# Splitting one gate column earlier and loading the second half of the output weights inside the gated stage

## The chip, the cores and the metric

The kernel runs on one core of a Trainium2 chip. The metric is the device time of one execution in microseconds, as the median of the runs. The engines that matter are TensorE (PE, with its weight loads as PEld), VectorE (DVE), ScalarE (ACT), GpSimd (POOL) and SyncE (SP, which here only issues transfers). Each works through its own list of instructions in order and waits on semaphores for the others.

## The reference, cut to what matters

One encoder layer over two sequences of 512 tokens with 1024 features, all in float32. The part that the change touches:

```python
y = jax.nn.gelu(lax.map(one_seq, u))
y_ssm = y * jax.nn.sigmoid(y @ w_glu + b_glu)
...
mixed = jax.nn.sigmoid(g_att) * y_att + jax.nn.sigmoid(g_ssm) * y_ssm
x = x + mixed @ w_out
h2 = rms_norm(x, ln2)
return x + jnp.square(jax.nn.relu(h2 @ w_up)) @ w_down
```

## The kernel before

Float32 matrices are multiplied as three products of rounded parts: each operand is kept as a high part (a cast on ACT) and a low part (the remainder, a subtraction on DVE). Making both from a raw tile is called a **split** here; a 256 KB piece (128 x 512) takes one ACT and one DVE instruction.

The **gated stage** (the loop over `u`, 2 to 15) makes `mixed`, transposed, in 16 units: `u = 2m + s` for eight columns `m` of 128 features, counted from 0, and two sequences `s`. For a unit, `product_of` runs 24 matmuls on PE against column `m` of `w_glu` (from unit 4 on; the first four products are made in the attention stage), `gate_out` (ACT, L723) applies the sigmoid, `mixed` (DVE, L728 and L729) multiplies and adds, `gated_states` (DVE, L710 and L711, with a sigmoid L707 on ACT for the later columns) prepares the next unit, and `parts_of` splits the result (ACT L733, DVE L734) into `mixT`. Three accumulators rotate among the products.

Beside this the stage makes two kinds of weights ready. `column_half(c, i)` loads half of column `c` of `w_glu` (SP, L682) into a `c_raw` buffer and splits it (ACT L683, DVE L684) into `gc_hi` and `gc_lo`; there are two buffers of each, so column `c` takes the place of column `c - 2`. `row_piece` loads one of the eight row pieces of a half of `w_out` (SP, L1170), also into one of the same two `c_raw` buffers (named `w_raw`), and splits it (ACT L1171, DVE L1172) into `w_rows`. `load_gates(m)` has POOL issue two 512 KB loads for a later column. Within the stage the order of PE, ACT, DVE, POOL and SP is that of the code.

Behind the stage come the **output products**: `out_half(x1, sq, t, b)` runs 24 matmuls of a token tile against half `b` of `w_rows`, DVE adds the input row (L1238), and `norm_of` (ACT L1255, POOL L1257 and L1258, DVE L1259, which needs `ln2_bc`) and `turn_of` (transposes on PE, L1273) prepare the up projection. PE runs half 0 for both sequences first, then half 1 for both, then the first transposes. Half 1 of `w_rows` is loaded and split at the head of this part, through three `w_raw` buffers of the pool `rn2`, into `slot_a`, where the gated stage keeps the state rows (`yT`) of columns 4 to 7. Two pieces of `w_up` (`f_raw`, L1247 to L1249) go through the same three buffers after that. Here only PE's order is that of the code; a scheduler sets the other engines' order.

Of the kernel before, what the change touches and what calls it, by code (L numbers as in the profile page):

```python
# [12 lines left out]
F32 = mybir.dt.float32  # L13
# [6 lines left out]
P = 128  # L20
D = 1024
# [3 lines left out]
KT = D // P  # L25
NSEQ = 2
HALF = 512
# [36 lines left out]
def hybrid_layer(ctx, tc, x, rel, onehot, w_qkv, w_ug, vectors, lam, coefs, w_glu, w_out, ln2,  # L64
                 w_up, w_down, out):
    nc = tc.nc
    V, S, PE, GP, SP = nc.vector, nc.scalar, nc.tensor, nc.gpsimd, nc.sync
# [58 lines left out]
    def slot(pool):  # L126
        return [pool.tile([P, KT, HALF], F32R, tag=f"act{i}", name=f"act{i}") for i in range(2)]


    slot_a = opers.enter_context(tc.tile_pool(name="slot_a", bufs=1, side="right", reuse_waits="tile"))  # L130
# [5 lines left out]
    cpool = cpool_cm.__enter__()  # L136
# [12 lines left out]
    columns = [("u", U_BLK + c) for c in range(KT)] + [("a", GA_BLK + c) for c in range(KT)] + [("s", GS_BLK + c) for c in range(KT)]  # L149
# [525 lines left out]
    def glu_pieces(m, pool, eng=V):  # L675

        def piece(i):
            if i == 0:
                glu_w[m] = [pool.tile([P, KT, P], F32R, tag=tag, name="g" + tag) for tag in ("c_hi", "c_lo")]
            hi, lo = [q[:, i * KT // 2:(i + 1) * KT // 2, :] for q in glu_w[m]]  # L680
            raw = cpool.tile([P, KT // 2, P], F32, tag="c_raw", name="c_raw")
            SP.dma_start(raw, w_glu[m][:, i * KT // 2:(i + 1) * KT // 2, :])  # L682
            S.copy(hi, raw)  # L683
            return lambda: eng.tensor_tensor(lo, raw, hi.bitcast(F32), op=ALU.subtract)  # L684

        return [lambda i=i: piece(i) for i in range(2)]

    def load_gates(m):
        tiles = [p.tile([P, NTOK], F32, tag=tag, name=name) for p, tag, name in
                 ((wq, "c_hi", "ga"), (wq, "c_lo", "gs"), (evp, "ev", "at"))]  # L690
        glu_in[m] = tiles
        for t_, scr in zip(tiles[1:], (gs_scr, mix_scr)):
            GP.dma_start(t_, scr[m])
# [3 lines left out]
    def column_half(c, i):  # L697
        pieces.setdefault(c, glu_pieces(c, cpool))[i]()()
# [5 lines left out]
    def gated_states(u, pool, tag):  # L704
        m, s, (ga, gs, at) = sides(u)
        if (GS_BLK + m, s) not in sigmoids:
            S.activation(gs, gs, AF.Sigmoid)  # L707
        yy = pool.tile([P, HALF], F32, tag=tag, name="yy")
        halves = [q[:, m % 4].bitcast(F32).rearrange("p (t s k) -> p t s k", t=T, s=NSEQ)[:, :, s, :] for q in yT[m // 4]]
        V.tensor_add(yy.rearrange("p (k t) -> p t k", t=T), *halves)  # L710
        V.tensor_mul(gs, gs, yy)  # L711

    def product_of(u):
        m, s = divmod(u, 2)
        ps = acc()
        for k in range(KT):
            for _ in glu_step(ps, glu_w[m], k, s):
                pass
        glu_ps[m, s] = ps

    def gate_out(u):
        m, s, (ga, gs, at) = sides(u)
        S.activation(ga.rearrange("p (k t) -> p k t", t=T), glu_ps[m, s].rearrange("p (t k) -> p k t", t=T), AF.Sigmoid,  # L723
                     bias=bglu_sb[:, m:m + 1])

    def mixed(u):
        m, s, (ga, gs, at) = sides(u)
        V.tensor_mul(ga, ga, gs)  # L728
        V.tensor_add(ga, ga, at)  # L729

    def parts_of(u):
        m, s, (ga, gs, at) = sides(u)
        S.copy(mixT[s][0][:, m, :], ga)  # L733
        V.tensor_sub(mixT[s][1][:, m, :], ga, mixT[s][0][:, m, :].bitcast(F32))  # L734
# [430 lines left out]
    wpool_cm = tc.tile_pool(name="wpool", bufs=1, side="right", reuse_waits="tile")  # L1165
    wpool = wpool_cm.__enter__()

    def row_piece(w, half, k, raw):

        SP.dma_start(raw, w_out[half, :, k])  # L1170
        S.copy(w[0][:, k], raw)  # L1171
        V.tensor_sub(w[1][:, k], raw, w[0][:, k].bitcast(F32))  # L1172

    w_rows = [slot(wpool), None]
    mixT = [slot(slot_c), slot(slot_d)]
    with tc.tile_pool(name="glu", bufs=1, reuse_waits="tile") as gpool, \
            tc.manual_schedule(engines={ET.PE, ET.Activation, ET.DVE, ET.Pool, ET.SP}):
        parts_of(0)
        parts_of(1)
        load_gates(2)  # L1180
        for u in range(2, 2 * KT):
            m, s = divmod(u, 2)
            if u > 3:
                product_of(u)
                gate_out(u)
            mixed(u)
            if u + 1 < 2 * KT:
                gated_states(u + 1, gpool, "yy")
            parts_of(u)
            if s == 0 and m + 1 < KT:  # L1190
                if m > 2:
                    column_half(m + 1, 1)
                elif m == 1:
                    row_piece(w_rows[0], 0, 0, cpool.tile([P, HALF], F32, tag="c_raw", name="w_raw"))
            if s == 1:
                if m + 2 < KT:
                    if m > 1:
                        column_half(m + 2, 0)
                    load_gates(m + 2)
            if s == 1 and m < 7:  # L1200
                row_piece(w_rows[0], 0, m, cpool.tile([P, HALF], F32, tag="c_raw", name="w_raw"))
            if u == 14:
                row_piece(w_rows[0], 0, 7, cpool.tile([P, HALF], F32, tag="c_raw", name="w_raw"))
    wq_cm.__exit__(None, None, None)
    evp_cm.__exit__(None, None, None)
    cpool_cm.__exit__(None, None, None)
# [3 lines left out]

    t4p_cm = tc.tile_pool(name="t4p", bufs=1, reuse_waits="tile")
    t4p = t4p_cm.__enter__()
    w_rows[1] = slot(slot_a)
    b0, b1, t23 = mixT[0], mixT[1], slot(slot_b)
    t4 = [t4p.tile([P, 4, HALF], F32R, name=f"t4_{i}") for i in range(2)]
    B11, B21 = [[q[:, k:k + 4, :] for q in b0] for k in (0, 4)]
# [5 lines left out]
    first = []  # L1222
    with tc.tile_pool(name="rn2", bufs=2, reuse_waits="tile") as rn2:
        ln2_bc = rn2.tile([P, D], F32, name="ln2_bc", bufs=1)
        SP.dma_start(ln2_bc, ln2.to_broadcast([P, D]))
        for k in range(KT):
            row_piece(w_rows[1], 1, k, rn2.tile([P, HALF], F32, tag="w_raw", name="w_raw", bufs=3))

        def rows_of(sq, t):
            return slice((sq * 4 + t) * P, (sq * 4 + t + 1) * P)  # L1230

        def out_half(x1, sq, t, b):
            ps = acc()
            for k in range(KT):
                mm3(ps, [q[:, k, t * P:(t + 1) * P] for q in mixT[sq]], [q[:, k, :] for q in w_rows[b]],
                    k == 0, k == KT - 1)
            xs = x1[:, b * HALF:(b + 1) * HALF]
            V.tensor_add(xs, ps, xs)  # L1238

        def load_rows_of(sq, t):  # L1240
            x1 = rn2.tile([P, D], F32, tag="x1", name="x1")
            SP.dma_start(x1, x[rows_of(sq, t), :])
            return x1
# [66 lines left out]
        xb, owed = [], None  # L1310
        order.enter_context(tc.manual_schedule(engines={ET.PE}))
        x1s = [load_rows_of(sq, 0) for sq in range(NSEQ)]
        for sq in range(NSEQ):
            out_half(x1s[sq], sq, 0, 0)
        ws = [up_parts(0, i, *[fpre.tile([P, 4, P], F32R, tag=tag, name=tag) for tag in ("f_hi", "f_lo")]) for i in range(2)]
# [27 lines left out]
    with tc.tile_pool(name="up", bufs=2, reuse_waits="tile") as fp:  # L1343
# [43 lines left out]
        for r in range(NPAIR):  # L1387
            raw = fp.tile([P, 4, 4, P], F32, tag="u_raw", name="u_raw")
# [202 lines left out]
```

## Time and profile before

| | |
|---|---|
| median of 3 runs | 1502.4 us (1500.92 to 1504.12) |
| profiled execution | 1503.71 us |
| its span | 1501.9 us |
| granted TensorE clock, mean | 0.998 |
| ACT busy | 761.7 us (51%) |
| POOL busy | 212.6 us (14%) |

The profile is of one execution; its span runs from the first to the last recorded instruction. A row of the timeline has the start, the duration, the engine, the line, the operation with its output and inputs, and, in brackets, how long the engine idled just before and what ended that. A row of the stage sums has a stretch of the span, then the busy time and the number of instructions of each engine in it, the granted clock, the mean busy share of the 16 DMA engines and what they moved in GB/s. SPq rows are transfers that SP issues. Matmuls overlap, so a matmul's duration is longer than the distance to the next one.

### The profile page before, as it was taken

The numbers are of one execution on the slowest core, as the hardware profiler recorded it, in microseconds if no ns is written. First come the engines' busy times: TensorE is split into PE (matmuls) and PEld (weight loads), VectorE is DVE, ScalarE is ACT, GpSimd is POOL, SyncE is SP. The second block draws the span as 40 slices with busy tenths as digits, with TensorE's granted clock in tenths as the row PEclk, the third lists the DMA queues.
The fourth block names the chain that finished last, engine by engine and source line by source line (L and its number), as shares of the span: only waits on it lengthen the run. The fifth ranks groups of instructions, "written<-read, shape, count | busy, mean of one in ns | idle before, by whom it ended". The sixth has DMA issues, their size and how long they took to land.

```text
span 1501.9 us, 22138 instructions
## 1 busy us (share of the span) xinstructions
PE 1453.4 (97%) x8074; PEld 1230.0 (82%) x8074; DVE 1106.8 (74%) x1989; ACT 761.7 (51%) x1362; POOL 212.6 (14%) x372
## 2 busy tenths in 40 slices
PE   6999999999999999999999989999999999999998
PEld 4888888888999888887787868888888888888787
DVE  7998859976646888887975478777777588575653
ACT  6777852235536777775334254445555443433332
POOL 3133341002232443222100000000000000000000
PEclk9999999999999999999999999999999999999999
DMA  4455469229731445275544234444443794454441
GB/s 174 140 169 168 160 208 345 107 100 344 287 132 36 155 135 183 88 252 170 185 135 162 92 115 159 155 154 154 155 154 126 267 352 132 153 182 154 126 123 60
DMA packets 103165, 249.69 MB, mean 166 GB/s; under 512 B 12266, under 2 KB 23786, under 8 KB 103056
## 3 DMA queue, kind: packets, MB, share of 16 engines
q1 hardware_dynamic: 60528, 140.07, 28.7%
q0 software_dynamic: 16896, 53.53, 10.3%
q10 hardware_dynamic: 25632, 54.67, 9.7%
q8 instruction: 64, 1.05, 0.3%
q14 instruction: 45, 0.37, 0.1%
HBM read 173.74 MB, written 90.21 MB: 176 GB/s over the span
## 4 chain that ended last, share of the span: by engine, by line
PE 78%; DVE 8%; ACT 4%; DMA 4%; issue 3%; POOL 1%; ACTq 0%; SPq 0%; DVEq 0%; POOLq 0%
PE acc L185 14%; PE bank L117 13%; PE bank L118 13%; PE bank L116 13%; PE acc L813 4%; PE acc L123 3%; PE acc L117 2%; PE acc L118 2%; PE acc L116 2%; PE sps L547 2%; PE po L896 2%; PE sps L864 1%; PE tps L880 1%; PE sps L645 1%; DMA fac<-rs_scr 1%
## 5 line engine op out<-in xcount | busy, mean ns | idle before, releaser
L185 PE MATMUL acc<-act,c_hi 128*128 128x512 f32 x768 | 249.6, 400 | 1.0 <-DVE act L304 1.0
L117 PE MATMUL bank<-b_lo,a_hi 128*128 128x512 f32 x448 | 174.6, 390 | 1.6 <-DVE b_lo L1460 1.6
L118 PE MATMUL bank<-b_hi,a_lo 128*128 128x512 f32 x448 | 174.3, 389 | 0.0
L116 PE MATMUL bank<-b_hi,a_hi 128*128 128x512 f32 x448 | 173.5, 389 | 0.0
L185 PEld LDWEIGHTS acc<-act,c_hi 128*128 128x128 f32 x768 | 142.2, 189 | 29.1 <-DVE act L304 2.4
L185 PE MATMUL acc<-act,c_lo 128*128 128x512 f32 x384 | 152.5, 397 | 0.0
L1459 ACT CAST a_hi<-d_a 128x1024 fp32r<-128x1024 f32 x56 | 59.0, 1054 | 179.7 <-PE bank L117 176.4
L116 PE MATMUL bank<-act,act 128*128 128x512 f32 x368 | 144.1, 391 | 4.9 <-ACT act L1349 4.9
L117 PE MATMUL bank<-act,act 128*128 128x512 f32 x368 | 143.7, 391 | 0.0
L118 PE MATMUL bank<-act,act 128*128 128x512 f32 x368 | 143.7, 391 | 0.0
L1460 DVE TENSOR_TENSOR a_lo<-d_a,a_hi 128x1024 fp32r<-128x1024 f32 x56 | 68.5, 1224 | 99.9 <-ACT a_hi L1459 99.9
L813 PE MATMUL acc<-w_hi,act 128*128 128x256 f32 x512 | 116.2, 295 | 0.0
L117 PEld LDWEIGHTS bank<-b_lo,a_hi 128*128 128x128 f32 x448 | 84.1, 188 | 20.1 <-DVE b_lo L1460 2.6
L116 PEld LDWEIGHTS bank<-b_hi,a_hi 128*128 128x128 f32 x448 | 84.1, 188 | 17.5
L118 PEld LDWEIGHTS bank<-b_hi,a_lo 128*128 128x128 f32 x448 | 84.1, 188 | 17.3
L813 PEld LDWEIGHTS acc<-w_hi,act 128*128 128x128 f32 x512 | 87.0, 189 | 3.7
L874 ACT ACTIVATE p<-p,nmx 128x257 f32<-128x257 f32 (+1 forms) x128 | 72.1, 563 | 31.2 <-DVE nmx L868 30.2
L116 PEld LDWEIGHTS bank<-act,act 128*128 128x128 f32 x368 | 69.4, 189 | 19.7 <-ACT act L1349 5.3
L123 PE MATMUL acc<-act,gc_hi 128*128 128x512 f32 x256 | 82.6, 401 | 1.8 <-ACT gc_hi L683 1.8
L185 PEld LDWEIGHTS acc<-act,c_lo 128*128 128x128 f32 x384 | 72.4, 189 | 14.0 <-DVE c_lo L176 0.5
L118 PEld LDWEIGHTS bank<-act,act 128*128 128x128 f32 x368 | 69.4, 189 | 14.9 <-DVE act L1350 0.4
L117 PEld LDWEIGHTS bank<-act,act 128*128 128x128 f32 x368 | 69.5, 189 | 14.3
(328 smaller groups left out, 3434.4 us busy)
## 6 DMA issues: line engine op xcount, KB each, us to landing
d_a<-a_scr SPq DMA_DIRECT2D x56, 512.0 KB, 3.6
u_raw<-in_w_up_dram SPq DMA_DIRECT2D x32, 512.0 KB, 5.1
a_scr<-t ACTq DMA_DIRECT2D x64, 256.0 KB, 4.8
k<-in_w_down_dram SPq DMA_DIRECT2D x32, 512.0 KB, 6.4
c_raw<-in_w_ug_dram SPq DMA_DIRECT2D x48, 256.0 KB, 3.7
a_scr<-a ACTq DMA_DIRECT2D x46, 256.0 KB, 2.1
ct_scr<-ctab POOLq DMA_DIRECT2D x16, 576.0 KB, 3.7
ctab_in<-ct_scr POOLq DMA_DIRECT2D x16, 576.0 KB, 7.6
```

The lines of the kernel that those rows point to most:

```text
L116: PE.matmul(ps, a[0], b[0], start=first, stop=False)
L117: PE.matmul(ps, a[0], b[1], start=False, stop=False)
L118: PE.matmul(ps, a[1], b[0], start=False, stop=last)
L123: PE.matmul(ps, w[wi][:, k, :], rows[yi], start=k + p == 0, stop=k == KT - 1 and p == 2)
L185: PE.matmul(ps, w[wi][:, k, :], hT[s][hi][:, k, :], start=n == 0, stop=n == 3 * KT - 1)
L547: PE.matmul(ps[:, i * P:(i + 1) * P], bm[:, ri, g, :], u_sb[:, gp * SH + g, :], start=True, stop=True)
L645: PE.matmul(o, ctab[:, g0 % SI + g, ri, 0:T * CH], st[:, ri, g].rearrange("p s k -> p (s k)"), start=False, stop=ri == 1)
L813: PE.matmul(self.ps, hT[sq][act][:, k, col:col + P], w[:, k % 4, :], start=i == 0, stop=i == 3 * KT - 1)
L874: S.activation(p, p, AF.Exp, bias=self.nmx[:, h:h + 1], scale=-1.0, accum_out=self.sums[:, h, self.qb:self.qb + 1])
L896: PE.matmul(self.po, vv, self.hl[i][part], start=i + part == 0, stop=i == self.nkb - 1 and part == 1)
L1459: S.copy(hi, src)
L1460: V.tensor_sub(lo, src, hi.bitcast(F32))
```

## The change

Column 4, the fifth, is loaded and split in units 3 and 4 instead of 5 and 6; columns 5 to 7 keep their units. The eight row pieces of half 0 move from units 2, 3, 5, 7, 9, 11, 13 and 14 to units 7 to 14, one in each, behind the column's half. Half 1 of the output weights is loaded by the gated stage: pieces 0 to 3 into two tiles of the pool's `c_hi` and `c_lo` buffers, which held a column, issued in unit 13; pieces 4 and 5 through the two small buffers in unit 14, pieces 6 and 7 through them behind that. `w_rows[1]` is taken from `slot_a` in unit 14, and piece 0 is split there, the others behind the last unit. The load of `ln2_bc` moves behind the first loads of `x`.

```diff
-    def row_piece(w, half, k, raw):
-
+    def row_load(half, k, raw):
         SP.dma_start(raw, w_out[half, :, k])
+        return raw
+
+    def row_split(half, k, raw):
+        w = w_rows[half]
         S.copy(w[0][:, k], raw)
         V.tensor_sub(w[1][:, k], raw, w[0][:, k].bitcast(F32))
...
+        columns = {u: (4 + i // 2, i % 2) for i, u in enumerate((3, 4, 7, 8, 9, 10, 11, 12))}
+        late_raw = []
+
+        def small_piece(half, k):
+            return row_load(half, k, cpool.tile([P, HALF], F32, tag="c_raw", name="w_raw"))
+
         for u in range(2, 2 * KT):
...
             parts_of(u)
-            if s == 0 and m + 1 < KT:
-                if m > 2:
-                    column_half(m + 1, 1)
-                elif m == 1:
-                    row_piece(w_rows[0], 0, 0, cpool.tile([P, HALF], F32, tag="c_raw", name="w_raw"))
-            if s == 1:
-                if m + 2 < KT:
-                    if m > 1:
-                        column_half(m + 2, 0)
-                    load_gates(m + 2)
-            if s == 1 and m < 7:
-                row_piece(w_rows[0], 0, m, cpool.tile([P, HALF], F32, tag="c_raw", name="w_raw"))
+            if s == 1 and m + 2 < KT:
+                load_gates(m + 2)
+            if u in columns:
+                column_half(*columns[u])
+            if 7 <= u < 14:
+                row_split(0, u - 7, small_piece(0, u - 7))
+            if u == 13:
+                last = small_piece(0, 7)
+                for tag in ("c_hi", "c_lo"):
+                    pair = cpool.tile([P, 2, HALF], F32, tag=tag, name="w_raws")
+                    for i in range(2):
+                        late_raw.append(row_load(1, len(late_raw), pair[:, i]))
             if u == 14:
-                row_piece(w_rows[0], 0, 7, cpool.tile([P, HALF], F32, tag="c_raw", name="w_raw"))
+                row_split(0, 7, last)
+                late_raw += [small_piece(1, k) for k in (4, 5)]
+                w_rows[1] = slot(slot_a)
+                row_split(1, 0, late_raw[0])
+        for k in range(1, KT):
+            row_split(1, k, late_raw[k] if k < 6 else small_piece(1, k))
...
-    w_rows[1] = slot(slot_a)
...
-        SP.dma_start(ln2_bc, ln2.to_broadcast([P, D]))
-        for k in range(KT):
-            row_piece(w_rows[1], 1, k, rn2.tile([P, HALF], F32, tag="w_raw", name="w_raw", bufs=3))
...
         x1s = [load_rows_of(sq, 0) for sq in range(NSEQ)]
+        SP.dma_start(ln2_bc, ln2.to_broadcast([P, D]))
```

The three places below are from ACT and SP. First ACT at the head of the gated stage, from the cast of unit 2's part on, before:

```order
L733 CAST act_8417<-ga 128x512
L1171 CAST act_8415<-w_raw 128x512
L733 CAST act_8419<-ga 128x512
L1171 CAST act_8415<-w_raw 128x512
L723 ACTIVATE ga<-acc,vec 128x512
L733 CAST act_8417<-ga 128x512
L723 ACTIVATE ga<-acc,vec 128x512
L733 CAST act_8419<-ga 128x512
L683 CAST gc_hi<-c_raw 128x512
```

And in the changed kernel:

```order
L733 CAST act_8417<-ga 128x512
L733 CAST act_8419<-ga 128x512
L683 CAST gc_hi<-c_raw 128x512
L723 ACTIVATE ga<-acc,vec 128x512
L733 CAST act_8417<-ga 128x512
L683 CAST gc_hi<-c_raw 128x512
L723 ACTIVATE ga<-acc,vec 128x512
L733 CAST act_8419<-ga 128x512
L723 ACTIVATE ga<-acc,vec 128x512
```

The two casts of row pieces (L1171) are gone from here, and the two casts of column 4 (L683) stand around `gate_out(4)`, the first L723, where the first of them stood behind `gate_out(5)`.

SP from the last load of a column (L682) to the loads of `f_raw`, before; L1242 loads `x`, L1225 `ln2_bc`:

```order
L682 DMA c_raw<-in_w_glu_dram 128x512
L1170 DMA w_raw<-in_w_out_dram 128x512 x2
L1225 DMA ln_bc<-in_ln_dram 128x1024
L1170 DMA w_raw<-in_w_out_dram 128x512 x3
L1242 DMA x_9000<-in_x_dram 128x1024
L1170 DMA w_raw<-in_w_out_dram 128x512 x3
L1242 DMA x_9002<-in_x_dram 128x1024
L1170 DMA w_raw<-in_w_out_dram 128x512 x2
L1247 DMA f_raw<-in_w_up_dram 128x512 x4
```

And in the changed kernel, where `w_raws` are the two tiles in the column's buffers and the lines are L1169 (row pieces), L1252 (`x`), L1323 (`ln2_bc`) and L1257 (`f_raw`):

```order
L682 DMA c_raw<-in_w_glu_dram 128x512
L1169 DMA w_raw<-in_w_out_dram 128x512 x3
L1169 DMA w_raws<-in_w_out_dram 128x512 x4
L1169 DMA w_raw<-in_w_out_dram 128x512 x2
L1252 DMA x_8997<-in_x_dram 128x1024
L1252 DMA x_8999<-in_x_dram 128x1024
L1169 DMA w_raw<-in_w_out_dram 128x512 x2
L1323 DMA ln_bc<-in_ln_dram 128x1024
L1257 DMA f_raw<-in_w_up_dram 128x512 x4
```

Six of the eight loads of half 1 now stand ahead of the first load of `x`, and `ln2_bc` stands behind all eight.

ACT at the end of the gated stage, from unit 14's part on, before (L723 is `gate_out(15)`, `act_8952` is half 1 of the output weights):

```order
L733 CAST act_8417<-ga 128x512
L1171 CAST act_8415<-w_raw 128x512
L723 ACTIVATE ga<-acc,vec 128x512
L733 CAST act_8419<-ga 128x512
L1171 CAST act_8952<-w_raw 128x512 x8
L1248 CAST f_hi<-f_raw 128x512
```

And in the changed kernel, where `act_8924` is half 1:

```order
L733 CAST act_8417<-ga 128x512
L1174 CAST act_8415<-w_raw 128x512
L1174 CAST act_8924<-w_raws 128x512
L723 ACTIVATE ga<-acc,vec 128x512
L733 CAST act_8419<-ga 128x512
L1174 CAST act_8924<-w_raws 128x512 x3
L1174 CAST act_8924<-w_raw 128x512 x4
L1258 CAST f_hi<-f_raw 128x512 x2
```

One cast of half 1 moved ahead of `gate_out(15)`; the other seven follow the last part as before. From there on the order of every engine is the same, but for the add, the `f_raw` splits and the store of the first `x` rows, which change places by one or two.

## The prediction, on record before the changed kernel ran

> **What bounds the kernel now.** The page was read first (shares of the engines, then the chain that ended last), then the sums by stage around the code that moves, then the timeline of TensorE (PE) there, then the queues that it waits for.
>
> ```profile
> PE 1453.4 (97%) x8074; PEld 1230.0 (82%) x8074; DVE 1106.8 (74%) x1989; ACT 761.7 (51%) x1362; POOL 212.6 (14%) x372
> core 0: us, PE busy (x) PEld busy (x) DVE busy (x) ACT busy (x) POOL busy (x), PEclk, DMA share, GB/s
> 708.79:730.55 21.76, 21.76 (x97) 17.82 (x95) 21.34 (x30) 7.37 (x13) 3.21 (x6) 1.00 0.56 188
> 730.55:741.64 11.09, 8.15 (x25) 5.52 (x25) 10.92 (x17) 5.00 (x10) 1.11 (x3) 0.85 0.68 213
> 741.64:779.76 38.12, 38.12 (x169) 31.53 (x168) 32.59 (x46) 16.97 (x29) 2.16 (x4) 1.00 0.40 132
> 779.76:790.64 10.88, 10.88 (x49) 9.01 (x48) 3.97 (x7) 3.17 (x5) 0.00 (x0) 1.00 0.59 191
> 790.64:804.77 14.13, 12.67 (x49) 8.47 (x47) 7.10 (x12) 5.39 (x9) 0.81 (x2) 1.00 0.68 220
> 806.00:884.00 78.00, 77.93 (x371) 64.40 (x372) 41.36 (x57) 26.27 (x46) 5.56 (x14) 1.00 0.24 88
> ```
>
> PE is busy for 97% of the span, so a change pays only where PE idles or runs slowly. In the gated stage and behind it that is 730.55 to 741.64 (8.15 of 11.09 busy, granted clock 0.85) and 790.64 to 806. Elsewhere there PE is gapless; in the first row VectorE (DVE) is nearly gapless too, 21.34 of 21.76.
>
> ```profile
> 730.32 0.39 PE L123 MATMUL acc<-act,gc_lo 128*128 128x512 f32 x1
> 731.31 0.73 PE L123 MATMUL acc<-act,gc_hi 128*128 128x512 f32 x2 [0.61 <-ACT gc_hi L683]
> 732.78 0.50 PE L123 MATMUL acc<-act,gc_lo 128*128 128x512 f32 x1 [0.73 <-DVE gc_lo L684]
> 736.56 0.73 PE L123 MATMUL acc<-act,gc_hi 128*128 128x512 f32 x2 [1.23 <-ACT gc_hi L683]
> 737.66 0.50 PE L123 MATMUL acc<-act,gc_lo 128*128 128x512 f32 x1 [0.36 <-DVE gc_lo L684]
> 779.08 0.61 PE L123 MATMUL acc<-act,gc_hi 128*128 128x512 f32 x2
> 779.76 0.39 PE L116 MATMUL acc<-act,act 128*128 128x512 f32 x1
> 797.22 0.49 PE L116 MATMUL acc<-act,act 128*128 128x512 f32 x1 [0.57 <-ACT act L1171]
> 805.98 1.09 PE L1273 MATMUL tps<-ident,rn_xn 128*128 128x128 f32 x8 [1.05 <-DVE rn_xn L1259]
> ```
>
> The first four waits are product u=8, the first that reads column 4: both halves of its split come late. From 779.08 to 779.76 three matmuls start, 0.2267 us each, so a product or an output half of 24 takes 5.44.
>
> **The change, part by part.** First, **column 4**. Its load stands behind row pieces that hold the two `c_raw` buffers:
>
> ```profile
> 720.38 0.33 SPq L682 DMA_DIRECT2D c_raw<-in_w_glu_dram  x1
> 732.75 1.01 SPq L682 DMA_DIRECT2D c_raw<-in_w_glu_dram  x2
> 719.67 0.69 DVE L1172 TENSOR_TENSOR act<-w_raw,act 128x512 fp32r<-128x512 f32 x1
> 713.12 0.94 SPq L1170 DMA_DIRECT2D w_raw<-in_w_out_dram  x2
> 742.07 0.69 DVE L1172 TENSOR_TENSOR act<-w_raw,act 128x512 fp32r<-128x512 f32 x1 [0.19 <-ACT act L1171]
> 742.68 0.69 DVE L728 TENSOR_TENSOR ga<-ga,gs 128x512 f32<-128x512 f32 x1
> 743.40 0.69 DVE L729 TENSOR_TENSOR ga<-ga,at 128x512 f32<-128x512 f32 x1
> 744.01 1.14 DVE L710 TENSOR_TENSOR yy<-act,act 128x512 f32<-128x512 f32 x1
> 745.19 0.69 DVE L711 TENSOR_TENSOR gs<-gs,yy 128x512 f32<-128x512 f32 x1
> 745.80 0.69 DVE L734 TENSOR_TENSOR act<-ga,act 128x512 fp32r<-128x512 f32 x1
> ```
>
> The second half is issued at 732.75, after product 8 should have begun. The change puts both loads where the two row loads stand at 713.12. DVE then decides: by the starts above a unit (L728 to L734) takes 3.73 of it and a split 0.61. From 719.67, where the first L1172 drops out, unit 3 with one split and unit 4 up to its split give 719.67 + 4.34 + 3.73 = 727.7, so column 4 is whole at 728.4, 2.1 before PE needs its first half at 730.55. Product 8's wait goes: eight products of 5.44 from 730.55 end at 774.08 instead of 779.76. **Gain 5.68**; bounds: nothing, if column 4 is still late, and 5.68.
>
> Part of that is a slow clock, which has a row of its own:
>
> ```profile
> 738.00:742.00 4.00, 4.00 (x12) 3.14 (x11) 3.81 (x6) 1.72 (x4) 1.08 (x2) 0.57 0.75 226
> 783.00:800.00 17.00, 15.54 (x62) 11.03 (x61) 7.41 (x11) 5.36 (x9) 0.00 (x0) 1.00 0.75 242
> ```
>
> After waits of at most 1.23 us each the clock was granted at 0.57 over 4 us, which costs 4 x 0.43 = 1.7 of the 5.68; the waits between 793 and 798 left it at 1.00. So a short wait that stays could cost 1.7 too, which is a rival below. The Trainium skill ("TensorE: Matmul & The Clock Gate", section "Why this matters for your kernels") asks only that PE has no gaps over about 3 us: by that rule no wait that stays here costs clock and that rival falls away; the row of 738 doesn't bear the rule out.
>
> Second, a **new wait on ScalarE (ACT)**: column 4's first cast now stands ahead of `gate_out(4)` and waits until product 5 has read column 2, whose buffer it takes. That is about 719.6 (730.55 less two products of 5.44, less one matmul).
>
> ```profile
> 722.82 0.68 ACT L723 ACTIVATE ga<-acc,vec 128x512 f32<-128x512 f32 x1
> ```
>
> Behind it stand `gate_out(4)` and the rest of ACT, and DVE and the accumulators wait for those; but `gate_out(4)` runs only at 722.82 now, behind casts of parts that wait for the late DVE. Cost 0; were that cover gone, 0.62, the cast itself.
>
> Third, the **row pieces of half 0** move to units 7 to 13, eight splits as before. Units 7 to 12 then take 3.73 + 1.22 = 4.95 of DVE, under 5.44. But DVE enters late, and column 5's second half shows it: 719.67 + 4.34 + 4.34 + 3.73 + 3.73 + 4.95 + 3.73 = 744.5, done at 745.2, while product 10 asks for it at 730.55 + 10.88 + 3.17 = 744.6. So 0.6 of wait. Its load starts when the first half's split ends, 740.2:
>
> ```profile
> DMA to landing us min/median/max: 2.6/3.1/3.3
> DMA to landing us min/median/max: 2.7/3.2/4.9
> gs<-gs_scr POOLq DMA_DIRECT2D x7, 512.0 KB, 3.6
> ```
>
> (First `c_raw`, then `w_raw`, issue to landing; last one of the two loads that POOL issues for a column, with its median.) With 3.1 and 0.6 of cast it is no later than DVE; with 4.9 the wait is 1.9. **Cost 0.7**, near the median; from 0.6 to 1.9. Later columns have the 0.5 a unit that DVE gains.
>
> Fourth, **half 1 of the output weights**. Now its loads wait for the stage to end, three buffers at a time, and PE catches up with them:
>
> ```profile
> SPq L1225 <- DVE ga L729: 12.8, 1, 12.8
> 783.61 1.28 SPq L1170 DMA_DIRECT2D w_raw<-in_w_out_dram  x3
> 786.79 0.62 ACT L1171 CAST act<-w_raw 128x512 fp32r<-128x512 f32 x1 [3.98 <-DMA w_raw<-in_w_out_dram]
> 799.60 0.62 ACT L1248 CAST f_hi<-f_raw 128x512 fp32r<-128x512 f32 x1 [1.63 <-DMA f_raw<-in_w_up_dram]
> 800.86 0.68 DVE L1238 TENSOR_TENSOR x<-acc,x 128x512 f32<-128x512 f32 x1
> 802.47 1.06 ACT L1255 ACTIVATE rn_xn<-x 128x1024 f32<-128x1024 f32 x1
> 804.64 1.29 DVE L1259 SCALAR_TENSOR_TENSOR rn_xn<-x,rs,ln_bc 128x1024 f32<-128x1024 f32 x1 [1.35 <-POOL rs L1258]
> ```
>
> Four output halves from 779.76 would end at 779.76 + 21.76 = 801.52; the transposes begin at 805.98. The excess of 4.46 is 3.25 of waits for half 1's splits (the fourth half ends at 804.77) and 1.21 for the norm chain, whose add (800.86) and square (802.47) stood behind `f_raw`'s splits. In the change pieces 0 to 3 load into the freed column buffers once product 13 is done (763.2 + 0.7), 4 and 5 by 775. Product 15 ends at 774.8; with piece 0's cast, `gate_out`, two mixes, cast and split (0.62 + 0.68 + 1.33 + 0.62 + 0.69) the last part is done at 778.7, and five splits of 0.61 end at 781.8. Pieces 6 and 7 wait for splits 4 and 5, so issue about 781.5 and land by 786.4 even with 4.9; their splits end by 788, and PE, which reaches half 1 at 774.8 + 10.88 = 785.7, asks for piece 6 at 789.7. `x`, `ln2` and `f_raw` go out between, by about 784; the norm chain (800.86 to 805.93, 4.2 without its late square) fits in the 5.44 of the fourth half. The one cast of half 1 ahead of `gate_out(15)` waits for product 15 and adds 0.62 to a part that PE reads only at the end of the second half, 785. **Gain 4.46**; bounds: nothing, if the loads land as late as the part allows, and 4.46.
>
> **Sum**: 5.68 - 0.70 + 4.46 = 9.4. The profiled execution took 1503.71 (span 1501.9) and would take 1494.3; the median of the runs is 1.3 below it, so 1493.0. From 806 on PE is gapless (77.93 of 78), with the same order on every engine, and the stage moves forward whole.
>
> **The rivals.**
>
> The load loop becomes the bound. In units 7 to 12 each half's load is issued only when the half before is split: landing plus 1.5 (cast, split, three handovers) a turn. At the median, 4.6, it hides under 5.44; at 4.9, the longest row, a turn is 6.4, and five turns from 740.2 end at 772.2 where product 14 asks at 766.4: the gated stage loses 5.8, all that it gained, and 1498.0 is left. For it: POOL's two 512 KB loads and a row piece share those units. Against it: DMA share 0.40 in 741 to 780, no `c_raw` over 3.3. 9%. The Trainium skill ("DMA: Bandwidth & Descriptors", section "Issuing engines are not separate DMA queues") says that transfers of all issuing engines interleave on the same 16 engines, which speaks for it; no row here parts that from the spread of 2.7 to 4.9.
>
> Slower: the same loop with landings above 5.8 us: five turns of 7.3 end at 776.7 and eat all 10.1. At 6.5, 1506. No row has it. 3%.
>
> Column 4 doesn't come early, because something ahead of its casts is later than DVE's count: only 4.46 is left, 1497.9. Its margin is 2.1. 4%.
>
> The wait that stays trips the clock as at 738: 1.7 more, 1494.7. The waits of 793 to 798 speak against it. 5%.
>
> A wait that these rows don't show gives most of it back, say behind 884 where the next stage starts: 1501. The same rows on every engine speak against it. 4%.
>
> **How the numbers follow.** The forecast holds 75%. The low end of the range is 1502.4 - 10.1 (nothing left of the 0.7) less 1.5, by which the runs lie apart from their median: 1490.8. The high end takes in the clock and the load loop for landings up to about 4.8, 1497.6; some 14% is left above it. Same means 1499.4 to 1505.4 (0.2%, about what a measurement of this kernel can tell): 4%, the last case; slower 3%; the other cases are faster, 93%.
>
> **What would show it.** Right: no PE wait for `gc_hi` at product 8 and a clock of 1.00 there; a wait of 0.5 to 1 near 744.5 for column 5; the first output product at 774 to 775.5; no waits for half 1, and transposes at 796 to 797. Wrong: gaps at units 9 to 14 that end with `c_raw` landing, a gap before `tps<-ident,rn_xn`, or 806 to 884 longer than 78.

## The result, and the profile after

The changed kernel took 1492.69 us (median of 4 runs, 1490.92 to 1494.04), against 1503.26 for the kernel before beside it: ratio 0.9927, 95% interval 0.9914 to 0.994. A second comparison (6 runs against 11) gave 1493.45 against 1502.85, ratio 0.994, interval 0.9925 to 0.9956. The forecast was 1493.0, with 1490.8 to 1497.6 as its range.

First the page of the changed kernel and its busy time by stretch; the columns are those of the prediction's first block.

```profile
PE 1448.4 (97%) x8074; PEld 1228.8 (83%) x8074; DVE 1105.0 (74%) x1989; ACT 760.9 (51%) x1362; POOL 212.5 (14%) x372
...
core 0: us, PE busy (x) PEld busy (x) DVE busy (x) ACT busy (x) POOL busy (x), PEclk, DMA share, GB/s
705.40:727.16 21.76, 21.76 (x98) 18.02 (x96) 21.35 (x30) 7.50 (x14) 3.14 (x6) 1.00 0.56 182
727.16:738.04 10.88, 10.88 (x50) 9.01 (x48) 10.71 (x16) 4.01 (x7) 1.16 (x3) 1.00 0.55 199
738.04:749.55 11.51, 11.04 (x49) 8.79 (x48) 11.34 (x17) 5.99 (x10) 1.07 (x2) 1.00 0.65 222
749.55:771.48 21.93, 21.93 (x98) 18.16 (x97) 20.19 (x30) 11.78 (x20) 1.07 (x2) 1.00 0.57 183
771.48:782.36 10.88, 10.88 (x49) 9.01 (x48) 7.38 (x13) 5.23 (x10) 0.00 (x0) 1.00 0.55 189
782.36:793.24 10.88, 10.88 (x49) 8.82 (x47) 4.51 (x7) 2.82 (x5) 0.81 (x2) 1.00 0.54 174
793.24:871.50 78.26, 77.93 (x371) 64.31 (x371) 41.83 (x58) 26.27 (x46) 5.54 (x14) 1.00 0.23 88
```

The second row is products 8 and 9, where PE was busy for 8.15 of 11.09 us at a clock of 0.85 before: now it is gapless at 1.00. Of the waits one is left in the gated stage (738 to 749.55), and the third and fourth output halves (782.36 to 793.24), which lost 3.25 before, are gapless. Now PE's timeline, at the anchors and at that wait.

```profile
699.80 0.27 PE L921 MATMUL tps<-ident,rsum 128*16 128x128 f32 x1 [0.35 <-DVE rsum L916]
...
740.76 0.61 PE L123 MATMUL acc<-act,gc_hi 128*128 128x512 f32 x2
741.84 0.50 PE L123 MATMUL acc<-act,gc_lo 128*128 128x512 f32 x1 [0.47 <-DVE gc_lo L684]
...
771.48 0.39 PE L116 MATMUL acc<-act,act 128*128 128x512 f32 x1
...
793.68 1.09 PE L1283 MATMUL tps<-ident,rn_xn 128*128 128x128 f32 x8 [0.28 <-DVE rn_xn L1269]
```

And the anchor of the kernel before:

```profile
703.19 0.27 PE L921 MATMUL tps<-ident,rsum 128*16 128x128 f32 x1 [0.35 <-DVE rsum L916]
```

The transposes of `rsum` are the last thing that PE does for the attention inside the gated stage, 5.60 us ahead of product 4 in both kernels, and no code ahead of them changed. Yet they ran at 703.19 in one profiled execution and at 699.80 in the other; over the profiled executions below they lie from 699.80 to 705.90, with the same code ahead. So 3.39 of the difference between the two spans is spread from ahead of the change, and **all that follows is measured from this row**: to the first output product (called R-O) and from there to the first transposes of the norm (O-N).

- R-O: 779.76 - 703.19 = 76.57 before, 771.48 - 699.80 = 71.68 after. Gain 4.89.
- O-N: 26.22 before, 22.20 after. Gain 4.02; four gapless output halves are 21.76.
- Together **8.91**, where the prediction summed 9.4.

### The profile page after: what moved, and what is told of

Read it like the earlier page. It is cut to its first block, busy times and chain, and to the rows that moved or that the text cites. A ratio compares the mean times of both kernels' runs of the same rounds, so it can differ in the third digit from the quotient of the medians.

```text
span 1489.1 us, 22131 instructions
## 1 busy us (share of the span) xinstructions
PE 1448.4 (97%) x8074; PEld 1228.8 (83%) x8074; DVE 1105.0 (74%) x1989; ACT 760.9 (51%) x1362; POOL 212.5 (14%) x372
## 3 DMA queue, kind: packets, MB, share of 16 engines
q8 instruction: 64, 1.05, 0.3%
## 4 chain that ended last, share of the span: by engine, by line
PE 76%; DVE 9%; issue 5%; ACT 4%; DMA 4%; POOL 1%; SPq 0%; ACTq 0%; DVEq 0%; POOLq 0%
PE acc L185 14%; PE bank L117 13%; PE bank L118 13%; PE bank L116 13%; PE acc L813 4%; PE acc L123 2%; PE acc L117 2%; PE acc L118 2%; PE acc L116 2%; PE sps L547 2%; PE po L896 2%; PE sps L864 1%; PE tps L880 1%; DVE pl L889 1%; DVE ya L906 1%
## 5 line engine op out<-in xcount | busy, mean ns | idle before, releaser
L116 PEld LDWEIGHTS bank<-act,act 128*128 128x128 f32 x368 | 69.4, 189 | 19.6 <-ACT act L1360 5.3
L185 PEld LDWEIGHTS acc<-act,c_lo 128*128 128x128 f32 x384 | 72.4, 189 | 13.9 <-DVE c_lo L176 0.4
```

The lines of the kernel that those rows point to most:

```text
L116: PE.matmul(ps, a[0], b[0], start=first, stop=False)
L185: PE.matmul(ps, w[wi][:, k, :], hT[s][hi][:, k, :], start=n == 0, stop=n == 3 * KT - 1)
```

## The experiments

The expectations call the stretch from product 4 to the first output product A, and the one from product 4 to the first transposes B: A is R-O less 5.60. They put A and B of the change at 65.91 and 88.11; from the `rsum` row they are 66.08 and 88.28.

| run | R-O | O-N | gained in the stage | ratio (interval) |
|---|---|---|---|---|
| before | 76.57 | 26.22 | | |
| the change, first and second time | 71.68, 71.60 | 22.20, 21.89 | 8.91, 9.30 | 0.9927 (0.9914 to 0.994), 0.994 (0.9925 to 0.9956) |
| 1 columns only | 71.67 | 26.94 | 4.18 | 0.9978 (0.9967 to 0.9989) |
| 2 half 1 only | 76.58 | 21.97 | 4.24 | 0.9963 (0.9949 to 0.9977) |
| 3 row pieces moved, column 4 not | 73.26 | 21.76 | 7.77 | 0.995 (0.9932 to 0.9967) |
| 4 column 4 moved, row pieces not | 73.88 | 21.76 | 7.15 | 0.9961 (0.9947 to 0.9974) |
| 6 row pieces a unit later | 71.01 | 22.14 | 9.64 | 0.9946 (0.9929 to 0.9962) |
| 7 `ln2` later | 71.71 | 21.77 | 9.31 | 0.9935 (0.9921 to 0.9949) |
| 8 both | 71.27 | 21.76 | 9.76 | 0.9936 (0.9921 to 0.9951) |
| 9 one buffer claimed, both in use | 71.57 | 22.05 | 9.17 | 0.9941 (0.992 to 0.9962) |
| 10 column 4's second half in unit 6 | 74.73 | 21.77 | 6.29 | one run |
| 11 the same in unit 7 | 79.04 | 21.76 | 1.99 | one run |
| 12 one buffer | 91.32 | 22.24 | -10.77 | 1.0064 (1.0047 to 1.0081) |

The stage's own gain, read from one execution, lies inside the interval of the times in every row that has one but the first (8.91, where the interval begins at 0.6% of 1503.26, 9.0).

### 1 and 2: the two halves of the change, each alone

Run 1 keeps the columns and row pieces of the change and loads half 1 as before:

```diff
-                for tag in ("c_hi", "c_lo"):
...
-                late_raw += [small_piece(1, k) for k in (4, 5)]
...
+        SP.dma_start(ln2_bc, ln2.to_broadcast([P, D]))
+        for k in range(KT):
+            row_split(1, k, row_load(1, k, rn2.tile([P, HALF], F32, tag="w_raw", name="w_raw", bufs=3)))
```

> Columns and row pieces of half 0 as in the change; half 1 of the output weights loaded behind the stage as before. Two stretches are read: A, from product 4's first matmul to the first output product (70.97 before, 65.91 in the change), and B, from the same start to the first transposes (97.19 and 88.11). Theory (the gains add up): A 65.9, and behind it the 26.22 of before, so B 92.1; time 5.1 below before, ratio 0.9966. Rival (the waits for half 1 came from the late column, so they shrink with it): A 65.9, B 89 to 90, time 7.5 to 9 below before.

Run 2 keeps the loads of half 1 and puts columns and row pieces back:

```diff
-        columns = {u: (4 + i // 2, i % 2) for i, u in enumerate((3, 4, 7, 8, 9, 10, 11, 12))}
+        columns = {u: (4 + i // 2, i % 2) for i, u in enumerate((5, 6, 7, 8, 9, 10, 11, 12))}
+        rows = {2: 0, 3: 1, 5: 2, 7: 3, 9: 4, 11: 5, 13: 6}
...
-            if 7 <= u < 14:
-                row_split(0, u - 7, small_piece(0, u - 7))
+            if u in rows:
+                row_split(0, rows[u], small_piece(0, rows[u]))
```

> Columns and row pieces of half 0 in the units of before; half 1 of the output weights loaded as in the change. Theory (the gains add up): A 71.0 with the four waits at product 8 and the clock of 0.57 near them, then the 22.20 of the change, B 93.2; time 4.0 below before, ratio 0.9973. Rival (half 1's loads in the stage push a wait into products 14 and 15 or the early output halves when the stage is late): A above 71.3 or B above 94, time less than 3 below before.

R-O is 71.67 in run 1, that of the change, and 76.58 in run 2, that of before; O-N of run 2 is 21.97. The two halves are separate, as the prediction had them: 4.90 of R-O and 4.25 of O-N make 9.15, and the change with both has 8.91 and 9.30. B is 98.55 - 5.60 = 92.95 in run 2, where 93.2 was expected. In run 1 it is 93.01, 0.9 more than expected, since O-N is 0.72 longer than before; in time run 1 is 3.5 below before where 5.1 was expected (its ratio of 0.9966 lies just outside the interval), run 2 is 5.7 below where 4.0 was. The window of run 1 behind its waits for half 1 shows what came on top of them (the columns are those of the stage sums):

```profile
795.60:799.30 3.70, 3.40 (x8) 2.45 (x9) 2.19 (x4) 1.48 (x3) 0.00 (x0) 0.54 0.48 137
```

The clock fell to 0.54 behind waits of at most 0.49 each, where waits of up to 0.57 left it at 1.00 in the kernel before. Over 3.7 us that costs 3.7 x 0.46 = 1.7; O-N grew by less, since the gap of 1.05 ahead of the transposes is gone. And run 2 shows the late column 4 again, in PE's timeline:

```profile
729.63 0.73 PE L123 MATMUL acc<-act,gc_hi 128*128 128x512 f32 x2 [0.60 <-ACT gc_hi L683]
731.12 0.50 PE L123 MATMUL acc<-act,gc_lo 128*128 128x512 f32 x1 [0.76 <-DVE gc_lo L684]
...
734.45 0.73 PE L123 MATMUL acc<-act,gc_hi 128*128 128x512 f32 x2 [0.77 <-ACT gc_hi L683]
736.01 0.57 PE L123 MATMUL acc<-act,gc_lo 128*128 128x512 f32 x1 [0.83 <-DVE gc_lo L684]
```

with the clock at 0.51 from 736.30 to 739.80.

### 3 and 4: which move frees column 4

Both have half 1 as in the change. Run 3 has only the first of run 2's edits (`columns` at 5 and 6), run 4 only the second (`rows`).

> As the change, but column 4 stays in units 5 and 6, where it stood before; the row pieces are behind it, from unit 7 on. Theory (the two loading buffers and VectorE's count decide, and the row pieces held both): by a timetable made from the durations of the trace product 8 waits 2.2 in three waits (0.6, 0.25, 1.36), A 67.5, B 89.7, time about 7.5 below before; 1.7 more of each if the clock drops as it did before. Rival (column 4's place in the order alone decides): the waits of before stay, A 71.0, B 93.2, time 4.0 below before.

> As the change, but the row pieces of half 0 stay in their units of before (2, 3, 5, 7, 9, 11, 13, 14), with column 4 in units 3 and 4. Theory (buffers and VectorE's count): no wait at product 8, but 2.4 at product 10 (0.2, 1.45, 0.76), A 67.7, B 89.9, time about 7.4 below before; 1.7 more if the clock drops. Rival (column 4's move alone brings the gain, the moved row pieces nothing): A 65.9 or less, B 88.1, time 9 to 10 below before.

Run 3's timeline of PE, at product 8:

```profile
731.54 0.51 PE L123 MATMUL acc<-act,gc_lo 128*128 128x512 f32 x1 [0.46 <-DVE gc_lo L684]
735.91 0.50 PE L123 MATMUL acc<-act,gc_lo 128*128 128x512 f32 x1 [1.08 <-DVE gc_lo L684]
```

And run 4's, at product 10:

```profile
742.63 0.51 PE L123 MATMUL acc<-act,gc_lo 128*128 128x512 f32 x1 [0.46 <-DVE gc_lo L684]
746.55 0.73 PE L123 MATMUL acc<-act,gc_hi 128*128 128x512 f32 x2 [1.31 <-ACT gc_hi L683]
747.55 0.50 PE L123 MATMUL acc<-act,gc_lo 128*128 128x512 f32 x1 [0.27 <-DVE gc_lo L684]
```

That the row pieces held the buffers shows in run 3's queue of SP: both loads of column 4 go out at once, 9.9 us behind `rsum`, though their place in the code is that of before, where they went out 17.2 and 29.6 behind it (720.38 and 732.75).

```profile
713.05 0.94 SPq L682 DMA_DIRECT2D c_raw<-in_w_glu_dram  x2
```

Both theories of buffers and VectorE's count hold within 0.6: A is 67.66 (67.5 expected) and 68.28 (67.7). Against run 2, with neither edit, the row pieces' move alone gains 3.32 of R-O, column 4's alone 2.70, and both 4.90 to 4.98; a part of each first step, up to 1.7, is the slow clock, which neither run has. Run 10 below has shorter waits than run 4 and the slow clock all the same, so the shares of the two moves are not settled more closely than that. **Neither move gives the gain alone**: with column 4 early and the row pieces where they were, the wait goes on to column 5, two products later.

### 5 to 8: the 0.8 and the 0.4 that were left

Run 5 is the changed kernel again. Run 6 moves the row pieces of half 0 to one unit later, run 7 moves the load of `ln2` behind two loads of `f_raw`, run 8 does both:

```diff
-            if 7 <= u < 14:
-                row_split(0, u - 7, small_piece(0, u - 7))
+            if 8 <= u < 13:
+                row_split(0, u - 8, small_piece(0, u - 8))
+            if u == 13:
+                for k in (5, 6):
+                    row_split(0, k, small_piece(0, k))
```

```diff
-        SP.dma_start(ln2_bc, ln2.to_broadcast([P, D]))
         for sq in range(NSEQ):
             out_half(x1s[sq], sq, 0, 0)
         ws = [up_parts(0, i, ...
+        SP.dma_start(ln2_bc, ln2.to_broadcast([P, D]))
```

> The changed kernel once more, as the measure for the three beside it. Read from the transposes of rsum (5.60 us ahead of product 4, on the same PE order) to the first output product 71.7 and to the first transposes of the norm 93.9, against 76.57 and 102.79 before. Theory (8.9 us gained in the stage, the rest of the first difference was spread in the code ahead of it): time 8.9 below before, ratio 0.994. Rival (the change also speeds up something ahead of the stage): transposes of rsum again near 700 in the profiled execution and ratio 0.992 or 0.993.

> As the change, with the row pieces of half 0 one unit later (units 8 to 12, two in 13, one in 14), so that VectorE has one split less ahead of column 5's second half. Theory (VectorE's count makes the wait of 0.63 at product 10): the wait is gone, first output product 70.9 behind the transposes of rsum, 0.8 earlier than in the change. Rival (the landing of column 5's second load makes it): the wait stays at 0.5 to 0.7, 71.7. Either way near 0.1% of the time, less than the comparison of times can tell.

> As the change, with the load of ln2 put behind the two loads of f_raw instead of ahead of them. Theory (f_raw lands late because 512 KB more stand ahead of it; its splits then delay the add, and so the norm): f_raw lands about 2 us earlier, its splits are done before the third output half ends, the gap of 0.44 ahead of the first transposes goes, 21.8 from the first output product to the transposes instead of 22.2. Rival (the loads of x and of the last row pieces hold it up, not ln2): f_raw's splits stay where they are and the gap of 0.4 stays; or ln2 itself now comes late and the gap grows.

> Both of the last two edits together. Theory (the gaps are separate): transposes of rsum to first transposes of the norm 92.7, 1.2 us less than in the change and 10.1 less than before; from there on nothing is left to gain in the stage. Rival (the earlier end of the gated stage makes the output weights or f_raw late instead): 93.3 or more.

Run 5 has 9.30 in the stage and `rsum`'s transposes at 701.15: the difference of 10.6 in the first comparison was the stage's 9 and spread.

Then the wait that is left, at column 5. VectorE's timeline of the changed kernel, at the split of column 5's second half:

```profile
741.10 0.68 DVE L684 TENSOR_TENSOR gc_lo<-c_raw,gc_hi 128x512 fp32r<-128x512 f32 x1
```

And run 6's, at the same split:

```profile
742.50 0.68 DVE L684 TENSOR_TENSOR gc_lo<-c_raw,gc_hi 128x512 fp32r<-128x512 f32 x1
```

Counted from `rsum` the split starts at 741.10 - 699.80 = 41.30 in the change and at 742.50 - 701.82 = 40.68 in run 6: 0.62 earlier, one split less. PE's wait is gone, and R-O is 71.01. But run 6 alone does not part the two causes, because its edit also frees the buffer: the load of this half goes out about 25 us behind `rsum` (the second of the two in run 6's row), against 37.08 in the change. SP in the changed kernel, and then in run 6:

```profile
736.88 0.33 SPq L682 DMA_DIRECT2D c_raw<-in_w_glu_dram  x1
```

```profile
722.74 4.66 SPq L682 DMA_DIRECT2D c_raw<-in_w_glu_dram  x2
```

What decides is the change's own timeline. There VectorE has no idle time ahead of the split (its row above has no bracket), and ACT's cast of this half was done at 740.13, a microsecond before it:

```profile
739.51 0.62 ACT L683 CAST gc_hi<-c_raw 128x512 fp32r<-128x512 f32 x1
```

In that execution it was VectorE's count. The landing is close behind. In run 7, with the same code here, the cast waited for it, and PE first for the cast (0.23), with the same delay in the end:

```profile
742.32 0.62 ACT L683 CAST gc_hi<-c_raw 128x512 fp32r<-128x512 f32 x1 [1.04 <-DMA c_raw<-in_w_glu_dram]
```

Run 7 is not as clear. The gap ahead of the first transposes is gone (O-N 21.77), but it is 0.44 in the first execution of the change and 0.13 in the second, and runs 3 and 4, with `ln2` where the change has it, have none either. `f_raw` lands after 6.6 us (median), against 7.5 and 6.8 in the two of the change: not the 2 us expected. The chain is plain, in the timelines of ACT and VectorE of the changed kernel:

```profile
787.22 1.22 ACT L1258 CAST f_hi<-f_raw 128x512 fp32r<-128x512 f32 x2 [4.41 <-DMA f_raw<-in_w_up_dram]
...
787.88 1.29 DVE L1259 TENSOR_TENSOR f_lo<-f_raw,f_hi 128x512 fp32r<-128x512 f32 x2 [3.79 <-ACT f_hi L1258]
789.09 0.68 DVE L1248 TENSOR_TENSOR x<-acc,x 128x512 f32<-128x512 f32 x1
```

The add of the third output half waits behind `f_raw`'s splits on VectorE, and the norm behind the add. Among the runs with `ln2` where the change has it the gap goes with that landing: medians of 7.3 to 7.5 (the change, runs 2, 9 and 12) come with delays of 0.2 to 0.5, medians of 6.6 to 6.9 with 0.12 or none (the change's second time, runs 3, 4, 10 and 11), and only run 6 has 0.37 at 6.9. So the gap can be absent with `ln2` in its place; what makes `f_raw` land late was not settled.

Run 8 has 9.76 in the stage, the most of all, 0.46 to 0.85 more than the change, not the full 1.2 that its theory gave (its R-O has 0.25 of delay at a later column). In time it can't be told from the change beside it (1493.2 and 1493.45): no version that beats the change measurably was found.

### 9 and 12: the price of the load loop

The rival with the largest price was the loop load, cast, split, next load. Run 9 meant to take one of the two buffers away by claiming it and never writing it:

```diff
+                one_buffer()
                 column_half(*columns[u])
```

> As the change, but with one loading buffer instead of two for the columns and the row pieces of half 0: each of these loads waits for the split of the one before it. Theory (the load loop, the rival of the prediction, has a price of landing plus 1.5 a load): two loads a unit take 9 us at a landing of 3.0 where PE needs 5.44, so PE waits from product 10 on for first and second halves of columns; by a timetable made of the trace's durations the stage loses 18 to 19 us, 25 at a landing of 3.6; slower than before by 8 to 15 us. Rival (loads alone in flight land faster, 2.5 or less, and the loop stays cheaper): 12 us or less lost, about as slow as before.

R-O is 71.57, and a column's load and the row piece behind it are still issued 0.6 apart (742.53 and 743.13): both buffers stayed in use, so this run says nothing of the loop and is one more execution of the change. Run 12 loads everything from unit 7 to 13 into one tile instead:

```diff
+            if u == 7:
+                one.append(cpool.tile([P, HALF], F32, tag="c_raw", name="w_raw"))
...
-                row_split(0, u - 7, small_piece(0, u - 7))
+                row_split(0, u - 7, row_load(0, u - 7, one[0]))
```

> As the change, but from unit 7 to unit 13 the column halves and the row pieces 0 to 6 of half 0 are all loaded into one buffer, so that each of these loads waits for the split of the one before it. Theory (the load loop, the rival of the prediction, has a price of landing plus 1.5 a load): two loads a unit take 9 us at a landing of 3.0 where PE needs 5.44, so PE waits from product 10 on, mostly for second halves of columns; by a timetable made of the trace's durations the stage loses 18 to 19 us, 25 at a landing of 3.6, and is 90 to 96 from the transposes of rsum to the first output product; slower than before by 8 to 15 us. Rival (loads alone in flight land in 2.5 or less, and the loop stays cheaper): 12 us or less lost, about as slow as before.

Run 12's queue of SP, in the timeline:

```profile
744.86 0.33 SPq L682 DMA_DIRECT2D w_raw<-in_w_glu_dram  x1
749.11 0.33 SPq L1169 DMA_DIRECT2D w_raw<-in_w_out_dram  x1
753.20 0.33 SPq L682 DMA_DIRECT2D w_raw<-in_w_glu_dram  x1
757.52 0.33 SPq L1169 DMA_DIRECT2D w_raw<-in_w_out_dram  x1
```

The answer on its tile `w_raw` from 740 to 790, issue to landing:

```profile
DMA to landing us min/median/max: 2.6/2.8/4.5
```

And PE's timeline, the second halves of columns 5, 6 and 7:

```profile
748.14 1.00 PE L123 MATMUL acc<-act,gc_hi 128*128 128x512 f32 x2 [3.50 <-ACT gc_hi L683]
...
765.12 0.91 PE L123 MATMUL acc<-act,gc_hi 128*128 128x512 f32 x2 [4.03 <-ACT gc_hi L683]
...
784.11 1.22 PE L123 MATMUL acc<-act,gc_hi 128*128 128x512 f32 x2 [5.93 <-ACT gc_hi L683]
```

From 744.86 to 757.52 are three turns of 4.22: landing 2.8 plus 1.4. The prediction's "landing plus 1.5" is the price of a turn. R-O is 91.32, 19.6 more than in the change, and the kernel is 0.64% slower than before, 9.6 us, inside the 8 to 15 that the theory gave. That the 18 to 19 of the theory came out too is in part luck: the three long waits delay PE by 3.66 + 4.19 + 6.09 = 13.9, and most of the rest is the clock, granted at 0.52 to 0.58 for 3.9 to 5.5 us behind each of them, which the expectation did not name. The rival's mechanism is real and dear. In the change it did not come about: two buffers share the loads, ACT waited for some of them (1.48 us at most in the first execution), but PE for none in that execution; run 7 shows how close the landing is.

### 10 and 11: when the clock falls

Run 10 puts column 4's second half into unit 6:

```diff
-        columns = {u: (4 + i // 2, i % 2) for i, u in enumerate((3, 4, 7, 8, 9, 10, 11, 12))}
+        columns = {u: (4 + i // 2, i % 2) for i, u in enumerate((3, 6, 7, 8, 9, 10, 11, 12))}
```

Run 11 puts `column_half(4, 1)` into unit 7, ahead of column 5's first half.

> As the change, but column 4's second half is loaded and split in unit 6 instead of unit 4. Theory: two waits at product 8 for its cast and its split, 0.9 and 1.4 us, in all about 2.2; first output product 73.1 behind the transposes of rsum; the granted clock stays at 1.00, because the waits that dropped it before added up to more than 3 us within 7. Rival (any wait over a microsecond here drops the clock): 0.57 for some 4 us behind product 8, 74.8.

> As the change, but column 4's second half is loaded and split in unit 7, just ahead of column 5's first. Theory (idle time within some 7 us adds up, long or short): one wait of 4 to 5 us at the middle of product 8 and one of 1.4 behind it, 5.9 in all, and then the clock at 0.57 for some 4 us, 1.7 more; first output product 78.5 behind the transposes of rsum. Rival (only several short waits in a row drop it): clock 1.00, 76.8.

Run 10's timeline of PE, at product 8:

```profile
732.92 0.73 PE L123 MATMUL acc<-act,gc_hi 128*128 128x512 f32 x2 [1.00 <-ACT gc_hi L683]
734.35 0.67 PE L123 MATMUL acc<-act,gc_lo 128*128 128x512 f32 x1 [0.70 <-DVE gc_lo L684]
```

The window behind them, and then run 11's long wait in its timeline of PE:

```profile
735.00:738.40 3.40, 3.40 (x11) 2.62 (x10) 3.37 (x5) 1.76 (x3) 1.07 (x2) 0.57 0.72 231
```

```profile
734.92 1.22 PE L123 MATMUL acc<-act,gc_hi 128*128 128x512 f32 x2 [4.40 <-ACT gc_hi L683]
```

The waits are near the timetable's (1.00 and 0.70 of idle time, 1.17 and 0.98 of delay against the pace of 0.2267 a matmul, 2.15 together where 0.9 and 1.4, about 2.2, were expected), and the theory of the clock fell: these two were enough to bring it to 0.57, and R-O is 74.73, the rival's number. Run 11 lost 0.5 more than its theory gave, with the clock at 0.52 from 737.0 to 741.6; its rival, that only several short waits in a row drop the clock, fell. Both runs are one execution each.

## Why the prediction was right

**Column 4 (gain 5.68): right, with its mechanism.** The prediction had column 4 whole at 728.4. The split of its second half in the changed kernel, in VectorE's timeline:

```profile
724.40 0.68 DVE L684 TENSOR_TENSOR gc_lo<-c_raw,gc_hi 128x512 fp32r<-128x512 f32 x1
```

It ends at 725.08, which is 728.47 when moved by the 3.39 between the two executions, 2.1 before product 8, as forecast. The term already counts the row pieces out of the way (the loads stand where theirs stood, and the first L1172 drops out), though it is called column 4's, and the pieces' new place is booked only as a cost. Runs 3 and 4 show how much hangs on both: of the 4.90 of R-O the row pieces' move alone brings 3.32, column 4's alone 2.70.

**ACT's new wait (cost 0): right.** In ACT's timeline the first cast of column 4 follows the cast of a part with no idle time, and `gate_out(4)` follows it. (The buffer's release works out at 719.4 from the prediction's own terms, not 719.6; the cast ran at 721.7, moved by 3.39, so nothing hangs on it.)

```profile
717.80 0.62 ACT L733 CAST act<-ga 128x512 fp32r<-128x512 f32 x1 [3.10 <-DVE ga L729]
718.33 0.62 ACT L683 CAST gc_hi<-c_raw 128x512 fp32r<-128x512 f32 x1
718.85 0.68 ACT L723 ACTIVATE ga<-acc,vec 128x512 f32<-128x512 f32 x1
```

**The wait at column 5 (cost 0.7): right in place, cause and size.** It is at the fifteenth matmul of product 10, at 741.84, which moved by 3.39 is 745.2, the time at which the prediction had the split done. The delay there is 0.63 against the pace of 0.2267. With what the next matmuls lost R-O is 71.68, where 5.60 and twelve gapless products give 70.89: 0.79. The change's own timeline shows that VectorE's count makes it, with the landing close behind, as the prediction had it.

**Half 1 (gain 4.46): the mechanism right, the size 0.1 to 0.4 too large.** The 3.25 of waits went. Of the 1.21 of the norm chain 0.77 came in the first execution and 1.08 in the second. The step that was mis-sized is "`x`, `ln2` and `f_raw` go out between, by about 784; the norm chain ... fits in the 5.44 of the fourth half": `f_raw` went out in time (779.74, which is 783.1 when moved by 3.39), but no landing was counted for it. It landed after 7.5 us, so that its splits again held up the add, and the transposes came at 797.07, moved likewise, just behind the 796 to 797 that were forecast.

**Sum and time.** 5.68 - 0.79 + 4.02 = 8.91, against 9.4. That the forecast of 1493.0 lies 0.3 from the first median and 0.5 from the second owes something to spread, since the code ahead of the stage varies by 6 us between executions. Behind the stage nothing came back: the stretch of 78.26 us in the stage sums begins 0.44 ahead of the transposes, and from them on PE is busy 77.97 of 78.02 us (793.68 to 871.70), with the same clock.

**The rivals.** The load loop has the price a turn that was given, but did not come about. The clock did not fall at the wait that stayed. The Trainium skill ("TensorE: Matmul & The Clock Gate", section "Why this matters for your kernels"), weighed there, asks only for no gaps over about 3 us; run 10 does not agree, where waits of 1.00 and 0.70 at product 8 were followed by a clock of 0.57.

## What to carry to other kernels

Where several transfers share a few loading buffers, a late one is moved by freeing the buffers ahead of it as much as by issuing it earlier: move both, and then look which transfer is now the last. An engine that runs gapless behind the pacing one (here VectorE, 21.35 of 21.76) can be counted instruction by instruction, and such a count gave the one wait left in the change to 0.1 us, and the sums of runs 3 and 4 to 0.6. For gains of a fraction of a per cent, measure from a row that lies behind all unchanged code, since here the code ahead, which nobody touched, differed by up to 6.1 us between executions, two thirds of the gain.

## What the runs showed of the hardware

**The granted clock fell behind short waits, and not by the longest wait or their plain sum.** It fell behind waits of 1.00 and 0.70 in run 10 and behind several of at most 0.49 in run 1; it held at 1.00 behind 0.46, 1.31 and 0.27 in run 4, of which the longest and the sum are above run 10's. PE's busy time in stretches of 3.4 us (the columns are those of the windows above), just ahead of a fall in the kernel before:

```profile
734.75:738.16 3.41, 1.81 (x7) 0.91 (x6) 3.38 (x5) 1.82 (x3) 0.00 (x0) 0.99 0.27 91
```

just ahead of the fall in run 1:

```profile
792.40:795.80 3.40, 2.13 (x6) 0.78 (x5) 1.72 (x3) 1.19 (x2) 0.00 (x0) 1.00 0.72 263
```

at the waits of run 3, where the clock stayed at 1.00:

```profile
733.00:736.40 3.40, 2.32 (x9) 1.33 (x9) 3.37 (x5) 1.63 (x3) 0.00 (x0) 1.00 0.18 69
```

and at those of run 4, where it also stayed, laid in two ways:

```profile
742.00:745.40 3.40, 2.77 (x11) 1.80 (x10) 3.37 (x5) 0.62 (x1) 0.00 (x0) 1.00 0.85 278
744.40:747.80 3.40, 1.81 (x7) 0.90 (x6) 3.37 (x6) 1.83 (x3) 0.00 (x0) 1.00 0.35 117
```

Ahead of a fall PE was busy for 1.81 and 2.13 of 3.4; it stayed at full clock with 2.32, and in run 4 with 1.81 or 2.77, as the stretch is laid. Behind short waits the slow stretch lasts about 3.4 to 3.7 us (735.00 to 738.40 in run 10, 795.60 to 799.30 in run 1). The Trainium skill ("TensorE: Matmul & The Clock Gate", section "What's actually happening") states that the clock is set by PE's activity in a free-running window of about 3.4 us. The length of the slow stretches agrees, and a window whose phase is chance would let the same waits cost 1.7 us in one execution and nothing in another, as run 4, with waits of like size, may show against the kernel before. No run shows the phase, so this stays an explanation that fits and is not shown. What is shown is that two waits of 1.00 and 0.70 can be enough, as in run 10.

**Landings were longer at the end of a burst of loads.** `f_raw` (256 KB) landed after 3.9 us (median) in the kernel before, and after 7.5 in the changed one, where two loads of `x`, two row pieces, `ln2` and three pieces of `f_raw`, 2.75 MB by the tiles' sizes, were issued within about 5 us from 775.82 on. The mean busy share of the 16 DMA engines was 0.83 from 777 to 787, against 0.51 while the kernel before waited for its first `f_raw` (795.89 to 799.60). A load through the one buffer of run 12 took 2.8 (median). Run 7, with `ln2` behind two of the pieces, has 6.6, so which of the loads in the burst counts for how much is open. The prediction's longest landing, 4.9, was no bound for the end of such a burst.
